# Second weighed one-hot row of every other group of eight tokens made by ScalarE, a token at a time

## The chip, the cores and the metric

The kernel runs on one core of one Trainium2 chip. The metric is the device time in microseconds of one execution, the median of the runs. Engines are called by the names of the profile: PE is TensorE (PEld its weight load), DVE is VectorE, ACT is ScalarE, POOL is GpSimd, SP is SyncE; ACTq and SPq are the queues from which ACT and SP issue transfers.

## The reference

Two blocks follow one another on 512 tokens of width 1024. What matters here is the last part of the second block, a layer of 16384 single-neuron experts, of which each token uses 128 (8 heads of 16):

```python
def peer_ffn(xn, w_q, sub_keys, u, v):
    ...
        best, pos = lax.top_k(cand, PEER_TOPK)
        expert = jnp.take_along_axis(cand_idx, pos, axis=-1)
        g = jax.nn.softmax(best, axis=-1)
        act = jax.nn.gelu(jnp.einsum('td,thkd->thk', xb, u[expert]), approximate=False)
        return jnp.einsum('thk,thkd->td', (g * act).astype(xb.dtype), v[expert])
```

An expert's number is `128 * key1 + key2`. The weight of an expert for a token is the sum of the token's `g` over its picks of that expert, and 0 where it has none.

## The kernel before

The 512 tokens stand in four tiles of 128. For one tile the experts' rows are gathered by indirect transfers. For the other three (`NDENSE`) the layer is computed densely: all 128 chunks of 128 experts, each as a projection (`u_task`, L1719 and L1722), a Gelu (L1731), a weight per expert and token (`weigh`, L1739) and a second product (`v_task`, L1766).

The weights of the dense tiles are a matrix of 16384 experts by 384 tokens, which `gate_matrix(i)` makes for tile i, four tokens at a time, and stores in the DRAM tensor `gate_d`. For a group of eight tokens, `rows` compares the picks' two keys with 0 to 127 on DVE (L1439, two instructions of 128x1024 in f16): for each pick (partition) and token a one-hot row of key 1 and one of key 2. `weighed` multiplies the rows of key 1 by the pick's weight (L1446). The weight is held as two f16 parts, `picks[i][:, 2]` and what f16 rounding left of it, `picks[i][:, 3]`, so there are two instructions, one for each part. `product` takes four tokens: for each, two matmuls of 128x128 (L1454, one for each part) add up the 128x128 matrix over key 2 and key 1 in PSUM. `store` copies the four matrices out of PSUM with two ACT instructions (L1463, called stores below) into staging tiles; after sixteen tokens two transfers bring these to `gate_d` (L1467, issued by ACT). There are 48 groups, 96 products, 192 stores and 48 transfers.

This runs in the background of the first projections: while PE does `u_task` for the first chunks, a generator is pumped. So PE's order is a projection (L1719, 16 matmuls in the trace, 8 rows in the order below), then a run of 4, 6 or 7 products, then the next projection. ACT takes the projection out of PSUM with one Gelu (L1731, `hid`). A scheduler fixes each engine's order when the program is built. In this phase projections and products take turns on the same four PSUM banks:

```python
BANKS = (dict(a=("a", 8)),
         dict(a=("a", 4), s=("s", 2), o=("o", 2), l=("o", 2), k=("o", 2)),
         dict(a=("a", 2), z=("z", 6)))
```

Roles that are not named there, `u` and `g` among them, use `a`. A projection or product that comes four places after another waits until ACT has emptied the bank. The one-hot rows use a tag of ten buffers (`sm.tile(..., tag="t", bufs=NT)`); a group holds three of them (key 2 and the two weighed parts) until PE has done its two products.

After the last store the first weights are read back (`load_gates`, L1695, issued by SP), and the dense layer goes on in other PSUM banks.

Of the kernel before, what the change touches and what calls it, by code (L numbers as in the profile page):

```python
# [7 lines left out]
F32 = mybir.dt.float32  # L8
# [4 lines left out]
AF = mybir.ActivationFunctionType  # L13
OP = mybir.AluOpType
# [155 lines left out]
def tile_kernel(ctx: ExitStack, tc: tile.TileContext, ins, out):  # L170
    nc = tc.nc
# [14 lines left out]
    def ps_tile(role="a"):  # L186
        tag, n = psum["roles"].get(role, psum["roles"]["a"])
        return psum["pool"].tile([128, 512], F32, tag=tag, bufs=n, name="ps")
# [101 lines left out]
    sm = ctx.enter_context(tc.tile_pool(name="sm", bufs=2))  # L290
# [547 lines left out]
    def second_block():  # L838
# [554 lines left out]
            def weights(i):  # L1393

                ex, best = picked.pop(i)
                ex = [ex[:, j] for j in range(2)]
                if i in idx:
                    nc.vector.scalar_tensor_tensor(out=idx[i].rearrange("p (h k) -> p h k", k=TOPK), in0=ex[0],
                                                   scalar=float(NKEY), in1=ex[1], op0=OP.mult, op1=OP.add)
                    g = gw[i].rearrange("p (h k) -> p h k", k=TOPK)  # L1400
                else:
                    g = sm.tile([128, PH, TOPK], F32, name="gwt", bufs=1)
                nc.vector.tensor_tensor(out=g, in0=best, in1=best[:, :, 0:1].to_broadcast([128, PH, TOPK]),
                                        op=OP.subtract)
                nc.scalar.activation(g, g, AF.Exp)
                sm8 = sm.tile([128, PH], F32, name="sm8", bufs=1)
                nc.vector.tensor_reduce(out=sm8, in_=g, axis=AX.X, op=OP.add)
                nc.vector.reciprocal(out=sm8, in_=sm8)
                nc.vector.tensor_tensor(out=g, in0=g, in1=sm8[:, :, None].to_broadcast([128, PH, TOPK]), op=OP.mult)
                if i in picks:  # L1410
                    p = ps_tile("g")
                    for j, x in enumerate((*ex, g)):
                        nc.tensor.transpose(p[:, j * 128:(j + 1) * 128], x.rearrange("p h k -> p (h k)"), ident)

                    x = picks[i]
                    nc.scalar.activation(x[:, :2], p[:, :256].rearrange("p (a b) -> p a b", b=128), AF.Copy)
                    nc.scalar.activation(x[:, 2], p[:, 256:384], AF.Copy, scale=WSCALE)
                    nc.vector.scalar_tensor_tensor(out=x[:, 3], in0=p[:, 256:384], scalar=WSCALE, in1=x[:, 2],
                                                   op0=OP.mult, op1=OP.subtract)
                    W.later(gate_matrix(i), name="gates")  # L1420

            def gate_matrix(i):

                k1, k2, *w = (picks[i][:, j] for j in range(4))
                full = [128, 4, 128, 2]
                keys = it16[:, None].to_broadcast(full)
                stage = []

                def wide(x, t0):
                    return x[:, t0:t0 + 8].rearrange("p (a b) -> p a b", b=2)[:, :, None, :].to_broadcast(full)  # L1430

                def row():
                    return sm.tile([128, 4, 128, 2], F16, tag="t", bufs=NT, name="oh")

                def rows(t0):

                    oh = [row() for _ in range(2)]
                    for x, k in zip(oh, (k1, k2)):
                        nc.vector.tensor_tensor(out=x, in0=keys, in1=wide(k, t0), op=OP.is_equal)  # L1439
                    return oh  # L1440

                def weighed(t0, oh):

                    parts = [row() for _ in w]
                    for x, y in zip(parts, w):
                        nc.vector.tensor_tensor(out=x, in0=oh[0], in1=wide(y, t0), op=OP.mult)  # L1446
                    return [oh[1], *parts]

                def product(t0, oh):
                    ps = ps_tile("g").rearrange("p (t n) -> p t n", n=128)  # L1450
                    for t in range(4):
                        a, b = divmod(t0 % 8 + t, 2)
                        for j in (1, 2):
                            nc.tensor.matmul(ps[:, t], oh[0][:, a, :, b], oh[j][:, a, :, b],  # L1454
                                             start=j == 1, stop=j == 2)
                    return ps

                def store(t0, ps):
                    if t0 % 16 == 0:
                        stage[:] = [W.pool.tile([128, 1024], F32, tag=tag, bufs=n, name="stage")  # L1460
                                    for tag, n in (("hi", SPLITS_AHEAD + 1), ("lo", SUBS_AHEAD + 1))]
                    for j in range(2):
                        nc.scalar.activation(  # L1463
                            stage[j].rearrange("p (n t) -> p t n", t=16)[:, t0 % 16:t0 % 16 + 4],
                            ps[:, :, j * 64:(j + 1) * 64], AF.Copy, scale=1.0 / WSCALE)
                        if t0 % 16 == 12:
                            nc.scalar.dma_start(gate_d[:, (128 * i + t0) // 16, j * 1024:(j + 1) * 1024], stage[j])  # L1467

                raw, oh, ps = {}, {}, {}
                for t0 in range(0, 128 + 12, 4):  # L1470
                    if t0 - 12 in ps:
                        store(t0 - 12, ps.pop(t0 - 12))
                    if t0 % 8 == 0 and t0 < 128:
                        raw[t0] = rows(t0)
                    if t0 - 4 in raw:
                        oh[t0 - 4] = weighed(t0 - 4, raw.pop(t0 - 4))
                    if 0 <= t0 - 8 < 128:
                        ps[t0 - 8] = product(t0 - 8, oh[(t0 - 8) // 8 * 8])
                    yield

            halves.extend([half(0), half(1)])
            n = [256]
# [70 lines left out]
            for word in PLAN.split():  # L1553
# [4 lines left out]
                else:  # L1558
                    name = word.rstrip("01234")
# [402 lines left out]
```

## Time and profile before

| | us |
|---|---|
| median of 3 runs (lowest to highest) | 3288.51 (3286.36 to 3288.88) |
| the profiled execution | 3287.23 |
| its span | 3285.5 |
| PE busy in the span | 3243.4 |
| DVE, ACT busy in the span | 2034.4, 1295.6 |

The span is the stretch from the first instruction to the last; 1.7 us of the profiled execution lie outside it. The granted clock was 0.997 of full over the span. All times of day below are microseconds from the start of the span. In a timeline a row that merges several instructions gives the first start, the time to the last end and their count, and in brackets the idle time of the engine ahead of it and what ended it.

### The profile page before, as it was taken

The numbers are of one execution on the slowest core, as the hardware profiler recorded it, in microseconds if no ns is written. First come the engines' busy times: TensorE is split into PE (matmuls) and PEld (weight loads), VectorE is DVE, ScalarE is ACT, GpSimd is POOL, SyncE is SP. The second block draws the span as 40 slices with busy tenths as digits, with TensorE's granted clock in tenths as the row PEclk, the third lists the DMA queues.
The fourth block names the chain that finished last, engine by engine and source line by source line (L and its number), as shares of the span: only waits on it lengthen the run. The fifth ranks groups of instructions, "written<-read, shape, count | busy, mean of one in ns | idle before, by whom it ended". The sixth has DMA issues, their size and how long they took to land. (4 is left out here: it accounts for less than half of the span.)

```text
span 3285.5 us, 47545 instructions
## 1 busy us (share of the span) xinstructions
PE 3243.4 (99%) x19335; PEld 2890.5 (88%) x19335; DVE 2034.4 (62%) x3979; ACT 1295.6 (39%) x2340; POOL 181.4 (6%) x132
## 2 busy tenths in 40 slices
PE   8999999999999999999999999999999999999999
PEld 7999999999888888888888988766789999999998
DVE  6545554433754555433466659988898888888443
ACT  5343332323533323232455543357433333333333
POOL 0000000000000000000000000000132222222000
PEclk9999999999999999999999999999999999999999
DMA  6222222222422222222332123356899988998442
GB/s 216 74 87 87 78 78 90 90 91 103 176 74 94 93 84 78 90 96 96 116 116 90 52 103 131 126 195 241 302 365 351 343 336 313 351 354 325 144 146 95
DMA packets 129947, 531.81 MB, mean 162 GB/s; under 512 B 9136, under 2 KB 60992, under 8 KB 73280
## 3 DMA queue, kind: packets, MB, share of 16 engines
q1 hardware_dynamic: 103520, 368.19, 31.2%
q0 software_dynamic: 18432, 134.23, 10.6%
q10 hardware_dynamic: 7776, 26.37, 2.0%
q8 instruction: 151, 2.47, 0.3%
q14 instruction: 68, 0.56, 0.1%
HBM read 501.48 MB, written 27.26 MB: 161 GB/s over the span
## 5 line engine op out<-in xcount | busy, mean ns | idle before, releaser
L143 ACT ACTIVATE hi<-raw 128x1024 fp32r<-128x1024 f32 x532 | 563.3, 1060 | 1396.5 <-PE ps L387 620.6
L151 DVE TENSOR_TENSOR lo<-raw,hi 128x1024 fp32r<-128x1024 f32 x532 | 650.8, 1224 | 744.8 <-ACT hi L143 741.2
L387 PE MATMUL ps<-xnh,hi 128*128 128x256 f32 (+2 forms) x2080 | 511.4, 305 | 0.0
L387 PE MATMUL ps<-xnl,hi 128*128 128x256 f32 (+2 forms) x2080 | 510.3, 305 | 0.0
L387 PE MATMUL ps<-xnh,lo 128*128 128x256 f32 (+2 forms) x2080 | 508.9, 304 | 0.0
L1766 PE MATMUL ps<-hi,hw 128*128 128x512 f32 x1536 | 428.4, 394 | 3.5 <-ACT hid L1731 2.8
L1722 PE MATMUL ps<-hn,hi 128*128 128x384 f32 x1600 | 409.5, 337 | 0.0
L387 PEld LDWEIGHTS ps<-xnh,hi 128*128 128x128 f32 x2080 | 338.9, 188 | 18.0
L387 PEld LDWEIGHTS ps<-xnh,lo 128*128 128x128 f32 x2080 | 339.4, 189 | 17.1
L387 PEld LDWEIGHTS ps<-xnl,hi 128*128 128x128 f32 x2080 | 338.5, 188 | 15.9
L1766 PEld LDWEIGHTS ps<-hi,hw 128*128 128x128 f32 x1536 | 288.5, 189 | 64.2 <-ACT hid L1731 3.4
L1636 POOL DMA_INDIRECT uv<-uv,idx x128 | 181.1, 1415 | 2842.6 <-DVE hn L1596 2328.6
L1722 PEld LDWEIGHTS ps<-hn,hi 128*128 128x128 f32 x1600 | 290.8, 188 | 4.3
L1722 PE MATMUL ps<-hn,lo 128*128 128x384 f32 x800 | 269.2, 337 | 0.0
L1766 PE MATMUL ps<-lo,hw 128*128 128x512 f32 x768 | 240.2, 393 | 0.0
L1766 PEld LDWEIGHTS ps<-lo,hw 128*128 128x128 f32 x768 | 145.0, 189 | 32.4
L1664 DVE SCALAR_TENSOR_TENSOR acc<-uv,dots,acc 128x1024 f32<-128x1024 f32 x127 | 163.0, 1284 | 3.2
L1672 DVE SCALAR_TENSOR_TENSOR uv<-uv,hnT 128x1024 f32<-128x1024 f32 x128 | 155.9, 1219 | 11.7 <-DMA uv<-uv,idx 11.7
L1719 PE MATMUL ps<-hn,raw 128*128 128x384 f32 x448 | 149.6, 490 | 5.5 <-ACT stage L1463 4.9
L1722 PEld LDWEIGHTS ps<-hn,lo 128*128 128x128 f32 x800 | 150.0, 188 | 0.1
L888 PE MATMUL ps<-x,hi 128*128 128x256 f32 x768 | 140.9, 287 | 4.0 <-ACT x L274 3.4
L1719 PEld LDWEIGHTS ps<-hn,raw 128*128 128x128 f32 x448 | 83.4, 190 | 63.3 <-ACT stage L1463 8.2
(353 smaller groups left out, 5036.8 us busy)
## 6 DMA issues: line engine op xcount, KB each, us to landing
raw<-ws SPq DMA_DIRECT2D x313, 1024.0 KB, 4.8
gate_d<-stage ACTq DMA_DIRECT2D x48, 512.0 KB, 3.5
gates<-gate_d SPq DMA_DIRECT2D x16, 1536.0 KB, 13.1
dm<-decay_m SPq DMA_DIRECT2D x8, 264.0 KB, 5.3
vb<-vbias SPq DMA_DIRECT2D x8, 256.0 KB, 5.6
dc<-decay SPq DMA_DIRECT2D x8, 256.0 KB, 5.4
uv<-uv,idx POOLq DMA_INDIRECT x128, 8.3
h<-ht SPq DMA_DIRECT2D x2, 544.0 KB, 5.0
```

The lines of the kernel that those rows point to most:

```text
L143: nc.scalar.activation(hi, raw[i], AF.Copy)
L151: nc.vector.tensor_tensor(out=lo, in0=r, in1=parts[i][0].bitcast(F32), op=OP.subtract)
L387: nc.tensor.matmul(t[:, :b - a], w[wi][:, off + k, :], x[k].t[xi][:, a:b], start=(k == 0 and n == 0), stop=(k == K - 1 and n == 2))
L888: nc.tensor.matmul(p, parts[wi][:, k, :], x[k][:, xi], start=(k == 0 and n == 0), stop=(k == K - 1 and n == 2))
L1636: nc.gpsimd.indirect_dma_start(out=t, out_offset=None, in_=ins["uv"], in_offset=bass.IndirectOffsetOnAxis(ap=idx[i][:, j:j + 1], axis=0))
L1664: nc.vector.scalar_tensor_tensor(out=acc, in0=v, scalar=dots[:, j:j + 1], in1=acc, op0=OP.mult, op1=OP.add)
L1672: nc.vector.scalar_tensor_tensor(out=u, in0=u, scalar=1.0, in1=hnT, op0=OP.mult, op1=OP.mult, accum_out=dots[:, j:j + 1])
L1719: nc.tensor.matmul(ps, w[0][:, k, :], tl["hn32"][k][:, :ND], start=k == 0, stop=k == KD - 1)
L1722: nc.tensor.matmul(ps, w[wi][:, k, :], tl["hn"][k][:, xi], start=(k == 0 and n == 0), stop=(k == KD - 1 and n == 2))
L1766: mm = nc.tensor.matmul(tl["acc"][t][b], h[:, hi, t * 128:(t + 1) * 128], w[vi][:, b * 512:(b + 1) * 512], start=(e == 0 and n == 0), stop ...
```

## The change

For every second group of eight tokens (`t0 % 16` is 8 when `weighed` is called with the group's first token) the second of the two multiplications leaves DVE. In its place ACT runs eight instructions, one for each token, on 128x128 elements that lie two apart, each a copy scaled by that token's column of weights: a scale that differs from partition to partition. The scale is read from `rest`, an f32 copy of the second weight part, which ACT makes once for each token tile. So 24 DVE instructions go and 192 + 3 ACT instructions come.

```diff
@@ -1422,6 +1422,8 @@
                 k1, k2, *w = (picks[i][:, j] for j in range(4))
+                rest = sm.tile([128, 128], F32, name="rest")
+                nc.scalar.activation(rest, w[1], AF.Copy)
                 full = [128, 4, 128, 2]
@@ -1442,8 +1444,13 @@
                 def weighed(t0, oh):
 
                     parts = [row() for _ in w]
-                    for x, y in zip(parts, w):
-                        nc.vector.tensor_tensor(out=x, in0=oh[0], in1=wide(y, t0), op=OP.mult)
+                    for n, (x, y) in enumerate(zip(parts, w)):
+                        if n and t0 % 16:
+                            for t in range(8):
+                                nc.scalar.activation(x[:, t // 2, :, t % 2], oh[0][:, t // 2, :, t % 2], AF.Copy,
+                                                     scale=rest[:, t0 + t:t0 + t + 1])
+                        else:
+                            nc.vector.tensor_tensor(out=x, in0=oh[0], in1=wide(y, t0), op=OP.mult)
                     return [oh[1], *parts]
```

The scheduler places the new instructions. Lines shift by seven: the stores are L1470 after the change, `hid` is L1738, the transfers are L1474, the new instructions L1450. Two places on ACT and one on DVE are shown.

The first is ACT's order in the third token tile, from the projection ahead of products 76 to 82 (counted from 0 over the three tiles) to the next one. Before, it read:

```order
L1731 ACTIVATE hid<-ps 128x384
L1463 ACTIVATE stage<-ps 128x4x64 x10
L1467 DMA gate_d<-stage 128x1024 x2
L1463 ACTIVATE stage<-ps 128x4x64 x2
L1731 ACTIVATE hid<-ps 128x384
```

With the change the same piece reads:

```order
L1738 ACTIVATE hid<-ps 128x384
L1470 ACTIVATE stage<-ps 128x4x64 x4
L1450 ACTIVATE oh<-oh,rest 128x128 x6
L1470 ACTIVATE stage<-ps 128x4x64 x2
L1450 ACTIVATE oh<-oh,rest 128x128 x2
L1470 ACTIVATE stage<-ps 128x4x64 x8
L1474 DMA gate_d<-stage 128x1024 x2
L1450 ACTIVATE oh<-oh,rest 128x128 x8
L1738 ACTIVATE hid<-ps 128x384
```

Eight of the new instructions stand between the first four stores and the last eight, and eight more behind these. Twelve stores became fourteen because PE now has all of the seventh product ahead of the next projection, where it had one of its eight matmuls.

The second is ACT's order in the first token tile, between the projections ahead of and behind products 15 to 21, with the change. Sixteen of the new instructions stand here, all behind the tenth store:

```order
L1738 ACTIVATE hid<-ps 128x384
L1470 ACTIVATE stage<-ps 128x4x64 x2
L1474 DMA gate_d<-stage 128x1024 x2
L1470 ACTIVATE stage<-ps 128x4x64 x8
L1450 ACTIVATE oh<-oh,rest 128x128 x4
L1470 ACTIVATE stage<-ps 128x4x64 x2
L1450 ACTIVATE oh<-oh,rest 128x128 x4
L1470 ACTIVATE stage<-ps 128x4x64 x2
L1474 DMA gate_d<-stage 128x1024 x2
L1450 ACTIVATE oh<-oh,rest 128x128 x8
L1738 ACTIVATE hid<-ps 128x384
```

Before, that stretch held sixteen stores and two pairs of transfers between its two `hid` rows, with nothing else between them.

The third is DVE's order near the end of the third token tile, with the change. Two comparisons and then two multiplications used to repeat for every group:

```order
L1441 TENSOR_TENSOR oh<-it_100,picks_104 128x1024 x2
L1453 TENSOR_TENSOR oh<-oh,picks_104 128x1024 x2
L1441 TENSOR_TENSOR oh<-it_100,picks_104 128x1024 x2
L1453 TENSOR_TENSOR oh<-oh,picks_104 128x1024
```

Every second pair of multiplications is now a single one, and nothing else moved.

## Rows read from the trace of the kernel before

**Rows 1.** The page's first part: busy time, share, instructions of PE.
```profile
PE 3243.4 (99%) x19335; PEld 2890.5 (88%) x19335; DVE 2034.4 (62%) x3979; ACT 1295.6 (39%) x2340; POOL 181.4 (6%) x132
```

**Rows 2.** Windows: the last two token tiles' products, and what follows to the dense layer.
```profile
2206.71:2294.31 87.60, 79.94 (x641) 56.64 (x640) 70.29 (x120) 60.05 (x130) 0.00 (x0) 1.00 0.61 231
2294.31:2318.04 23.73, 20.91 (x64) 12.08 (x64) 20.23 (x61) 15.40 (x28) 0.00 (x0) 0.98 0.83 285
```

**Rows 3.** Waits from 2140 to 2296: us in total, times, longest.
```profile
ACT hid L1731 <- PE ps L1719: 40.6, 15, 3.7
DVE oh L1439 <- PE ps L1454: 21.9, 13, 2.2
PE ps L1454 <- ACT stage L1463: 5.5, 17, 1.2
PE ps L1719 <- ACT stage L1463: 4.9, 12, 0.7
PE ps L1454 <- DVE oh L1439: 1.5, 6, 0.3
```

**Rows 4.** Timeline of PE, a run of six products and one of seven.
```profile
2206.71 2.46 PE L1454 MATMUL ps<-oh 128*128 128x128 f16 x40
...
2210.31 5.43 PE L1719 MATMUL ps<-hn,raw 128*128 128x384 f32 x16 [0.28 <-ACT stage L1463]
2215.57 2.49 PE L1454 MATMUL ps<-oh 128*128 128x128 f16 x40
...
2220.03 5.43 PE L1719 MATMUL ps<-hn,raw 128*128 128x384 f32 x16 [0.66 <-ACT stage L1463]
2225.30 2.42 PE L1454 MATMUL ps<-oh 128*128 128x128 f16 x39
```

**Rows 5.** Timeline of ACT beside the first of these runs.
```profile
2206.91 0.49 ACT L1731 ACTIVATE hid<-ps 128x384 f32<-128x384 f32 x1 [0.68 <-PE ps L1719]
2207.38 1.98 ACT L1463 ACTIVATE stage<-ps 128x256 f32<-128x256 f32 x4
...
2209.57 3.34 ACT L1463 ACTIVATE stage<-ps 128x256 f32<-128x256 f32 x7
...
2215.77 0.49 ACT L1731 ACTIVATE hid<-ps 128x384 f32<-128x384 f32 x1 [2.86 <-PE ps L1719]
```

**Rows 6.** Groups by line on ACT from 1600 to 2320: busy us, mean ns.
```profile
L143 ACT ACTIVATE hi<-raw 128x1024 fp32r<-128x1024 f32 x53 | 55.8, 1057 | 103.4 <-PE ps L888 60.3 <-PE ps L1276 23.7 <-DMA raw<-ws 9.5
...
L216 ACT ACTIVATE r<-ms,eps 128x8 f32<-128x8 f32 x4 | 1.2, 301 | 0.0
...
L1405 ACT ACTIVATE gwt<-gwt 128x128 f32<-128x128 f32 x3 | 0.9, 304 | 0.0
L1135 ACT ACTIVATE r<-r 128x8 f32<-128x8 f32 x4 | 0.8, 208 | 0.1
```

**Rows 7.** Timeline of ACT, three short instructions that follow one another.
```profile
2106.56 0.27 ACT L1417 ACTIVATE picks<-ps 128x128 f16<-128x128 f32 x1
2106.72 0.31 ACT L1405 ACTIVATE gwt<-gwt 128x128 f32<-128x128 f32 x1
2106.93 0.37 ACT L1176 ACTIVATE early<-ps 128x256 f32<-128x256 f32 x1
```

**Rows 8.** Groups by line on DVE from 1600 to 2400: the multiplications.
```profile
L1446 DVE TENSOR_TENSOR oh<-oh,picks 128x1024 f16<-128x1024 f16 x96 | 62.0, 686 | 0.0
```

**Rows 9.** Chain that ended last, in order of time, from the last stores on.
```profile
2296.53 2.64 DMA gate_d<-stage
...
2299.24 9.07 DMA gates<-gate_d
...
2308.34 2.55 DVE hid L1739 x6
...
2317.61 0.39 ACT hid L1731
...
2318.04 11.31 PE ps L1766 x36
```

## The prediction

> **What bounds the kernel now.** I began with the page's busy times: PE works 3243.4 of 3285.5 us [rows 1], so whatever makes PE wait longer goes straight to the end, and a change off PE can win back at most the 42 us in which it is idle. The change touches the phase in which the weights are made, so I asked for the windows of that phase. From 2206.71 to 2294.31, the last two token tiles, PE is busy 79.94 of 87.60 us, DVE 70.29, ACT 60.05 [rows 2]. DVE looks like the busier helper. The waits say otherwise: from 2140 to 2296 PE waits 5.5 + 4.9 = 10.4 us for ACT's stores, and 1.5 us for DVE's rows; DVE waits 21.9 us for PE to free its buffers, and ACT 40.6 us for projections to end [rows 3]. So DVE has room, and ACT delays PE although it is idle a third of the time. The timelines show why. ACT's stores come in a row behind each `hid`, one every 0.445 us ((3.34 - 0.67) / 6 with about 0.67 for the last), while PE fills four tokens' bank in 0.5 us (2.49 / 5). PE takes the banks in turn. With six products between projections, the next projection needs the bank of the third, which the sixth store empties; with seven, that of the fourth, and the eighth store. By the rows: `hid` at 2206.91, first store 0.47 later, sixth store five steps of 0.44 after that, 0.66 to end it, and the projection starts at 2210.31: 0.2 + 0.47 + 2.2 + 0.66 + 0.07 = 3.60 us after the run began, as seen. For seven products 0.2 + 0.47 + 3.08 + 0.73 = 4.48, seen 4.46 (2215.57 to 2220.03) [rows 4, 5]. Only the stores up to that one, which I call the deciding store, are on the path. The later ones run beside the projection (about 5.26 us from its start to the next run's, 2210.31 to 2215.57), and behind them ACT is idle for 2.86 us, which is the room that new work on ACT can have for nothing [rows 5].
>
> **What the change costs, part by part.** It takes 24 of the 96 multiplications from DVE, 24 x 62.0 / 96 = 15.5 us [rows 8]. PE hardly waits for DVE, so this is worth nothing, bounded by the 1.5 us.
>
> It gives ACT 192 scaled copies of 128x128. None is in the trace. The nearest row by shape and place is the Exp from SBUF to SBUF of 128x128, 304 ns [rows 6], after which the next instruction starts 0.21 us later (2106.72 to 2106.93) [rows 7]. That has no operand that differs by partition. What such an operand costs is seen on 128x8: 301 ns with one (L216, its bias), 208 without (L1135) [rows 6], 93 ns. So one lasts about 397 ns, and in a row of eight, of which each starts about 0.1 us ahead of the other's end, one comes every 0.30 us. The bounds: 0.16 us, the shortest step between rows of this size (L1417 to L1405, 2106.56 to 2106.72) [rows 7], and 0.40 us if nothing overlaps. I take 0.30, since the row nearest in kind carries that operand. [...]
>
> Now what of it lies on the path. In the order, I count the new instructions that stand ahead of the deciding store of each of the seventeen runs of products: none in eleven of them; 8 for products 9 to 14, 8 for 40 to 46, 8 for 53 to 59, 6 for 64 to 69, 8 for 76 to 82 (the first place shown), and 8 for 89 to 95. That is 46, and each holds up the stores behind it on ACT, and these the next projection: 46 x 0.30 = 13.8 us. In the other runs the new instructions stand behind the deciding store. There they cost nothing where they fit into the idle 2.86 us: eight take 2.4 us. At the second place shown sixteen stand there. Fourteen stores end 0.2 + 0.47 + 14 x 0.44 = 6.83 us after the run began, sixteen copies bring that to 11.63, while the projection ends at 4.48 + 5.26 = 9.74 and its `hid` could start at 9.94. So `hid` and the stores behind it are 1.7 us late, and the next run, of six, waits that long at its deciding store. With the delayed runs the projection starts later too, so that their eight behind (0.2 + 0.47 + 14 x 0.44 + 16 x 0.30 = 11.63 against 4.48 + 2.4 + 5.26 + 0.2 = 12.34) still fit. One spill therefore, 1.7 us.
>
> The rows that the copies read are DVE's, three groups ahead by the ten buffers, and DVE is lighter; I take no wait for them. The three copies into `rest` wait on ACT for DVE's second weight part. For the first two, `hid` waits behind them, and the cover is the run of projections ahead of the first products: with four banks PE notices nothing. Without that cover they would cost 2 to 4 us once. The first eight scaled copies have the same cover.
>
> Last, the end of the phase. PE waits for `hid` at 2318.04, and the chain leads back over the reading of the weights (9.07 us), the last transfer of stores at 2296.53, and ACT [rows 9]. From PE's last products on, that chain is 23.73 us long with PE busy 20.91 [rows 2], so nothing covers a delay. With the change the split of a weight piece (L143, `hi`) stands ahead of the store that this transfer waits for; before, it stood behind it. That is 1.06 us by its row [rows 6] if nothing else waits for it; I take 1.0, between 0 and 1.9 (the split and two stores more).
>
> The sum is 13.8 + 1.7 + 1.0 = 16.5 us, on the profiled execution's 3287.23: 3303.7. The median of the runs is 1.3 us above that execution; I round to 3304 us, 0.5% slower.
>
> **Rivals.** (a) *The copies fall into ACT's idle time or are short.* For it: 40.6 us of idle time on ACT [rows 3] against 192 x 0.16 = 31 us at the lower bound. Then 46 x 0.16 = 7.4 and no spill: 3295; with less on the path than I counted, 3290 to 3294. Against it: the operand's 93 ns, and the place of the 46.
> (b) *ACT becomes the bound throughout.* At 0.40 us a copy, 46 cost 18.4; the spill of sixteen grows to 3.3, and the runs for which eight just fitted spill by 0.1 to 1.1 each, about 2.2 together; with 1.9 at the end that is 25.8: 3313. For it: no row shows that copies with such an operand overlap, and elements two apart may cost more. In the stretch of 87.60 us [rows 2] ACT would have 60.05 us of old work and 112 of the copies, 45 us, 105 in all, in a stretch that (with 38 of the 46) the deciding stores alone would make 87.6 + 15.2 = 103 long; at 0.30 it is 94 of 99.
> (c) *Faster, because DVE sets the pace.* DVE is the busier of the two in rows 2, and its 21.9 us of waiting may be the loop of buffers between it and PE and no slack. Freed of 15.5 us it would run ahead, PE would find every run's rows and banks ready, and all of PE's waits in the phase would go, 5.5 + 4.9 + 1.5 = 11.9 us: 3275. It decides if the stores are late because products are, that is if ACT's `hid` has nothing queued behind it when PE waits. Against it: the 0.445 us step of the stores accounts for both runs to within 0.02 us.
>
> **How the numbers follow.** Chances: the forecast, steps of 0.25 to 0.35 us with the 46 on the path, 0.50; (b) 0.22; (a) 0.24; (c) 0.04. The forecast's own range is 3300 to 3307 (46 x 0.25 + 1 to 46 x 0.35 + 2.5 + 1). The range for 8 in 10 reaches from 3295, (a)'s lower bound, to 3313, (b)'s. About what a measurement of this kernel tells from no change is 0.2%, 6.6 us: 3282 to 3295. Half of (a), 0.12, lies within it; (c) alone lies below, 0.04; the rest, 0.84, is slower.
>
> **What would show it.** Right: the new rows (L1450) at 0.39 to 0.41 us each, some 0.30 apart; PE's waits for stores (10.4 us before) at about 25; runs of seven products such as 76 to 82 at 12 us in place of 9.7; those of six with the copies behind, 8.9 as before; DVE's waits for PE longer. Wrong: L1450 rows starting under 0.2 us apart; PE waiting for DVE's rows or for L1450 itself, which would mean that a product waits for its second part; `hid` late in nearly every run, which is (b); or a phase as long as before, which is (a).

## The result and the profile after

The changed kernel takes 3310.75 us (median; 3306.4 to 3311.46) against 3288.24 (3286.36 to 3288.88) for the kernel before beside it: ratio 1.0072, 95% interval 1.0059 to 1.0085. The forecast was 3304 with a range of its own, 3300 to 3307, and one for 8 in 10, 3295 to 3313; the median lies within the second and above the first. The profiled execution of the changed kernel took 3306.40 us with a span of 3304.6 and a granted clock of 0.996; the other runs have 0.993 to 0.994 and are 4 to 5 us longer.

First the page's busy times of the changed kernel, to be held against [rows 1]:

```profile
PE 3246.6 (98%) x19335; PEld 2892.9 (88%) x19335; DVE 2020.4 (61%) x3955; ACT 1348.3 (41%) x2535; POOL 187.4 (6%) x132
```

DVE lost 14.0 us, ACT gained 52.7, PE's busy time rose by 3.2 with the same matmuls. The last of these is the first sign of something that the forecast did not have.

The phase, as a window from the first product to the start of the last projections (1044 matmuls in both). Columns: stretch, its length, busy time of PE, of weight loads, DVE, ACT, POOL (instructions), granted clock, DMA share, GB/s. Before:

```profile
2140.78:2294.31 153.53, 140.63 (x1044) 97.45 (x1043) 128.82 (x310) 99.03 (x223) 0.00 (x0) 1.00 0.57 214
```

After:

```profile
2140.41:2313.51 173.10, 145.12 (x1044) 100.35 (x1042) 115.95 (x288) 149.50 (x408) 0.00 (x0) 0.97 0.50 190
```

This phase holds the loss: it is 19.57 us longer, where the two profiled executions as wholes differ by 19.17 (the end of the phase adds 0.8, and the stretches ahead of the phase and behind its end are 1.3 us shorter). PE's idle time went from 12.90 to 27.98 us, +15.1; its busy time rose by 4.5 at a clock of 0.97. The waits of the changed kernel from 2140 to 2316 (us in total, times, longest) say where the 15.1 come from:

```profile
DVE oh L1441 <- ACT oh L1450: 26.4, 7, 4.9
...
DVE oh L1453 <- ACT oh L1450: 19.7, 8, 3.2
PE ps L1461 <- ACT stage L1470: 16.5, 19, 1.9
ACT hid L1738 <- PE ps L1726: 10.7, 12, 2.2
...
DVE oh L1441 <- PE ps L1461: 6.7, 6, 1.9
PE ps L1726 <- ACT stage L1470: 6.6, 13, 1.9
...
PE ps L1461 <- ACT hid L1738: 2.7, 3, 2.0
...
PE ps L1726 <- ACT hid L1738: 1.8, 1, 1.8
...
PE ps L1461 <- DVE oh L1441: 0.3, 1, 0.3
```

PE waits for stores 16.5 + 6.6 = 23.1 us (10.4 in [rows 3]), for `hid` 4.5 (0.7 before), for DVE's rows 0.3 (1.8): 12.7 + 3.8 - 1.5 = 15.0. It never waits for a copy. DVE now waits 26.4 + 19.7 = 46.1 us for ACT to read its rows, and 6.7 in place of 21.9 for PE; almost none of it reaches the products.

One place, PE's timeline for products 40 to 46 (the run at 2215.57 of [rows 4]):

```profile
2221.69 2.50 PE L1461 MATMUL ps<-oh 128*128 128x128 f16 x40
2224.37 0.63 PE L1461 MATMUL ps<-oh 128*128 128x128 f16 x8 [0.18 <-ACT stage L1470]
2226.92 0.63 PE L1461 MATMUL ps<-oh 128*128 128x128 f16 x8 [1.92 <-ACT stage L1470]
2228.31 6.93 PE L1726 MATMUL ps<-hn,raw 128*128 128x384 f32 x16 [0.76 <-ACT stage L1470]
2235.07 1.10 PE L1461 MATMUL ps<-oh 128*128 128x128 f16 x16
```

And ACT's beside it:

```profile
2221.89 0.49 ACT L1738 ACTIVATE hid<-ps 128x384 f32<-128x384 f32 x1 [0.65 <-PE ps L1726]
2222.36 1.97 ACT L1470 ACTIVATE stage<-ps 128x256 f32<-128x256 f32 x4
2224.11 1.87 ACT L1450 ACTIVATE oh<-oh,rest 128x128 f16<-128x128 f16 x6
2225.84 1.03 ACT L1470 ACTIVATE stage<-ps 128x256 f32<-128x256 f32 x2
2226.66 0.70 ACT L1450 ACTIVATE oh<-oh,rest 128x128 f16<-128x128 f16 x2
2227.22 1.03 ACT L1470 ACTIVATE stage<-ps 128x256 f32<-128x256 f32 x2
```

The fifth and seventh store stand behind six and two copies; PE waits 1.92 us for the sixth store and 0.76 for the eighth. The run lasts 6.62 us in place of 4.46. Then the projection, with nothing to wait for, takes 6.93 us instead of 5.43. The window of that projection shows why: a granted clock of 0.77, where the phase before had 1.00.

```profile
2228.31:2235.07 6.76, 6.76 (x16) 3.85 (x17) 0.69 (x1) 4.76 (x14) 0.00 (x0) 0.77 0.40 158
```

The copies themselves, by their line (minimum, median and maximum in ns):

```profile
L1450 ACT ACTIVATE oh<-oh,rest x192: 397/427/466, 2111.2 to 2310.3; 128x128 f16<-128x128 f16 x192
```

A row of eight lasts 2.44 us, so one comes every (2.44 - 0.40) / 7 = 0.29 us.

### The profile page after: what moved, and what is told of

The parts are those of the page before. It is cut to its first block, busy times and chain, and to the rows that moved or that the text cites. A ratio compares the mean times of both kernels' runs of the same rounds, so it can differ in the third digit from the quotient of the medians.

```text
span 3304.6 us, 47730 instructions
## 1 busy us (share of the span) xinstructions
PE 3246.6 (98%) x19335; PEld 2892.9 (88%) x19335; DVE 2020.4 (61%) x3955; ACT 1348.3 (41%) x2535; POOL 187.4 (6%) x132
## 5 line engine op out<-in xcount | busy, mean ns | idle before, releaser
L143 ACT ACTIVATE hi<-raw 128x1024 fp32r<-128x1024 f32 x532 | 563.3, 1060 | 1405.3 <-PE ps L387 620.6
```

The costliest lines, as they stand in the source:

```text
L143: nc.scalar.activation(hi, raw[i], AF.Copy)
```

## The experiments

In this section each run's ratio is taken to the kernel before as it ran beside it. Theory 1 is the forecast's mechanism: a copy costs what it takes where it stands ahead of a deciding store (or of a `hid`) in ACT's order, and nothing elsewhere; the falls of the clock behind PE's longer waits were added to it from the trace after. Rival 1: ACT's occupancy costs, wherever the copies stand. Rival 2: products wait for second parts that come late. Rival 3: DVE sets the pace, so that its relief is worth something.

**Only the copies ahead.** (8 i + t0 // 16 numbers the 24 changed groups.)

```
-  if n and t0 % 16:
+  if n and t0 % 16 and 8 * i + t0 // 16 in (3, 11, 14, 17, 20, 23):
```

> Only six of the 24 multiplications go to ACT, those whose copies stand ahead of the deciding stores (46 of their 48 copies do, counted in the order); the other eighteen stay on DVE. Theory 1 (what stands ahead of a deciding store in ACT's row is paid in full, the rest is not): nearly the whole loss of the change, 46 x 0.29 = 13.3 us, about 3 us of falls of TensorE's clock behind the longer waits and 0.9 at the end: ratio 1.0052, about 3305 us (3301 to 3309). Rival 1 (ACT's occupancy costs, wherever the copies stand): a quarter of the measured 22.5 us, 3294 us, ratio 1.0017. Rival 2 (the products wait for second parts that come late): a quarter too, 3294 us, and waits of PE for the copies' rows.

Measured: 3304.55 us, ratio 1.0053 (1.0038 to 1.0067): a quarter of the copies makes three quarters of the loss. Rivals 1 and 2 fall by their number. The phase's window:

```profile
2140.89:2314.75 173.86, 150.54 (x1044) 102.61 (x1043) 125.38 (x302) 112.65 (x272) 0.00 (x0) 0.93 0.50 189
```

PE's idle time is 23.3 us, 10.4 more than before; its busy time is 9.9 more. So the clock took as much as the waits in this execution. The timeline of PE at products 40 to 46:

```profile
2221.96 0.63 PE L1461 MATMUL ps<-oh 128*128 128x128 f16 x8 [0.21 <-ACT stage L1470]
2224.50 0.62 PE L1461 MATMUL ps<-oh 128*128 128x128 f16 x8 [1.92 <-ACT stage L1470]
2225.89 8.49 PE L1726 MATMUL ps<-hn,raw 128*128 128x384 f32 x16 [0.77 <-ACT stage L1470]
```

The same waits as in the changed kernel, and behind them a projection of 8.49 us (clock 0.63 from 2225.89 to 2234.20), where the changed kernel had 6.93 at the same place. How deep the clock falls behind such waits differs from place to place and from run to run, while the waits repeat to 0.02 us. One line of this run's waits speaks for another cause:

```profile
PE ps L1461 <- DVE oh L1453: 4.0, 3, 1.9
```

Two of these three are 1.88 and 1.87 us long and stand at the places (2163.52 and 2248.03) where the changed kernel waits 1.87 and 1.86 for a store. ACT's store and DVE's row end there within 0.1 us of one another, so at these two places a store that comes earlier would have gained next to nothing without an earlier row.

**Only copies behind.**

```
-  if n and t0 % 16:
+  if n and t0 % 16 and 8 * i + t0 // 16 not in (0, 1, 3, 11, 14, 17, 20, 23):
```

> The counterpart: sixteen of the 24 multiplications go to ACT, those whose copies stand behind the deciding store of their run; the six ahead of it, and the first two of the first tile (whose copies stand ahead of the hid of a projection), stay on DVE. 128 copies, two thirds of ACT's new work. Theory 1: about the time of the kernel before, 3288 us (3285 to 3292), ratio 1.000 (to 1.001 for a spill behind sixteen copies). Rival 1 (occupancy): two thirds of 22.5 us, 3303 us, ratio 1.0046. Rival 3 (a lighter DVE is worth something): 16 x 0.65 = 10.3 us less on DVE, up to 3 us faster, 3285 us or less.

Measured: 3288.52 us, ratio 1.0008 (0.9999 to 1.0018). Two thirds of the new work on ACT cost nothing that can be measured. The phase's window:

```profile
2142.24:2296.84 154.60, 141.10 (x1044) 97.69 (x1042) 119.73 (x292) 134.66 (x352) 0.00 (x0) 1.00 0.56 213
```

ACT is busy 35.6 us longer than before, PE idle 0.6 longer, and the clock stays at 1.00. Rival 1 is refuted for this amount of work.

**DVE's relief alone.** This is an edit of the kernel before. In the odd groups the second part is left out, and PE uses the first one twice. Such a group holds two of the ten buffers in place of three, so DVE is relieved a little more than by the change.

```
-  parts = [row() for _ in w]
-  for x, y in zip(parts, w):
-      nc.vector.tensor_tensor(out=x, in0=oh[0], in1=wide(y, t0), op=OP.mult)
+  parts = [row() for _ in w[:1 if t0 % 16 else 2]] * (2 if t0 % 16 else 1)
+  for n, (x, y) in enumerate(zip(parts, w)):
+      if n and t0 % 16:
+          parts[1] = parts[0]
+      else:
+          nc.vector.tensor_tensor(out=x, in0=oh[0], in1=wide(y, t0), op=OP.mult)
```

> DVE's relief alone: in every other eight tokens the second part of the weight is left out (the first part's rows are multiplied twice, so PE has as many matmuls as before), DVE makes 24 multiplications fewer, and ACT gets nothing new. Theory 1: PE hardly waits for DVE, so about the time before, 3288 us (3286 to 3290), at best the 1.8 us that PE waited for DVE's rows. Rival 3 (DVE sets the pace of this phase): 24 x 0.65 us less, up to 3275 us, ratio 0.996. If the former holds, the change had nothing to win even with copies that cost nothing.

Measured: 3287.2 us, ratio 1.0007 (0.9998 to 1.0016). The change had nothing to win that can be measured, whatever its copies cost. DVE, 14 us lighter in the phase, waits longer for its buffers (21.9 us in [rows 3]; window 2140 to 2298):

```profile
DVE oh L1449 <- PE ps L1457: 35.4, 14, 3.7
...
PE ps L1457 <- ACT stage L1466: 7.4, 19, 1.1
```

PE waits 0.6 us for DVE's rows here (1.8 before) and 11.0 for stores (10.4 before).

**A shorter copy in the same place.** The second parts lose their weight (all are 0 or 1).

```
-  scale=rest[:, t0 + t:t0 + t + 1])
+  scale=1.0)
```

> The changed kernel with a constant 1.0 in place of the scale that differs by partition (the weight is left out of those second parts); all copies stay where they are. Theory 1: a copy lasts about 0.30 us and comes every 0.20 instead of 0.294 us, so 46 x 0.09 = 4.2 us less on the path, 0.7 less at the two hid, and shorter single waits (8 x 0.2 = 1.6 instead of 2.4 us), behind which the clock falls less often: 3302 us (3298 to 3307), ratio about 1.0045. If the copies cost by their place and not by their length, or wait on memory: as the changed kernel, 3310 us, ratio 1.007.

Measured: 3301.39 us, ratio 1.0043 (1.0029 to 1.0057). ACT's timeline for products 40 to 46 again:

```profile
2223.01 1.99 ACT L1470 ACTIVATE stage<-ps 128x256 f32<-128x256 f32 x4
2224.78 1.33 ACT L1450 ACTIVATE oh<-oh 128x128 f16<-128x128 f16 x6
2225.97 1.03 ACT L1470 ACTIVATE stage<-ps 128x256 f32<-128x256 f32 x2
2226.80 0.54 ACT L1450 ACTIVATE oh<-oh 128x128 f16<-128x128 f16 x2
```

The order is the same, a copy comes every (1.33 - 0.34) / 5 = 0.20 us, and the operand that differs by partition is the other 0.09 of 0.29, near the 93 ns between L216 and L1135 in [rows 6]. PE's wait in this run is 1.39 us in place of 1.92, and the projection behind it takes 5.43 us: no fall here. The execution has one fall, behind products 2 to 8 (a projection of 7.49 us).

**The copies beside the multiplications.** This too is an edit of the kernel before. DVE makes all multiplications, and ACT copies into a tile that nobody reads.

```
+  rest = sm.tile([128, 128], F32, name="rest", bufs=1)
+  nc.scalar.activation(rest, w[1], AF.Copy)
...
   nc.vector.tensor_tensor(out=x, in0=oh[0], in1=wide(y, t0), op=OP.mult)
+  if n and t0 % 16:
+      spare = sm.tile([128, 128, 2], F16, name="spare", bufs=1)
+      for t in range(8):
+          nc.scalar.activation(spare[:, :, t % 2], oh[0][:, t // 2, :, t % 2], AF.Copy,
+                               scale=rest[:, t0 + t:t0 + t + 1])
```

> DVE makes all 96 multiplications again, as before the change, and ACT makes the 192 scaled copies beside them, into a spare tile that nobody reads. The same new work on ACT, but no product waits for it. Since nothing hangs on the copies, they stand elsewhere in ACT's order: 26 of them ahead of deciding stores (3, 3, 4, 4, 4, 4, 4 in seven runs), where the change had 46, and never more than four in one run. Theory 1: 26 x 0.29 = 7.5 us and about 0.9 at the end, single waits of about 1 us longer, too short for falls of the clock: 3296 us (3293 to 3299), ratio 1.0025. Rival 1 (occupancy of ACT, wherever it stands): as the changed kernel, 3310, ratio 1.007. Rival 2 (products that wait for late second parts): 3288, ratio 1.000.

Measured: 3302.03 us, ratio 1.0049 (1.0035 to 1.0063), 17 us where theory 1 said 8 and the others 0 or 22. Rival 2 falls: no product reads these copies, PE waits for DVE's rows as long as before (1.7 us), and the copies cost 17. But my count for theory 1 was too low. The profiled execution is the shortest (3299.10 us), and its phase is 12.0 us longer than before; three of the other four have a granted clock of 0.995 against 0.997 and take 3302 to 3304 us. ACT's timeline shows what the count lacked:

```profile
2167.38 3.25 ACT L1452 ACTIVATE spare<-oh,rest 128x128 f16<-128x128 f16 x10
2170.50 0.46 ACT L1738 ACTIVATE hid<-ps 128x384 f32<-128x384 f32 x1
2170.87 1.05 ACT L1470 ACTIVATE stage<-ps 128x256 f32<-128x256 f32 x2
```

Ten copies stand behind the stores here, on top of single ones among them, and `hid` comes without a pause, 0.4 us later than its projection would have let it (PE's next run began at 2169.86, and a `hid` can follow 0.2 us after: 2206.71 and 2206.91 in [rows 4, 5]). ACT waits for projections 4.2 us in this phase (six times) where it waited 40.6 before [rows 3]. So the room behind the stores was used up in most runs, and late `hid` are a part of the loss; how much each part took I did not separate. Here occupancy does count, past the room that each run leaves; that a copy behind then costs as much as one ahead was not measured. (PE's longest wait for a store is 1.41 us, and the phase's clock is 1.00 in this execution. That waits of this length are too short for falls was an estimate; with the whole change on the quick stores, below, projections of 7.12 us stand behind waits of 1.18 and 1.24 us.)

**Fewer, faster or moved stores.** If stores decide, a kernel with quicker ones should beat both. The first try merges a product's two stores:

```
-  for j in range(2):
-      nc.scalar.activation(stage[j].rearrange("p (n t) -> p t n", t=16)[:, t0 % 16:t0 % 16 + 4],
-                           ps[:, :, j * 64:(j + 1) * 64], AF.Copy, scale=1.0 / WSCALE)
+  nc.scalar.activation(stage[0].rearrange("p (n t) -> p t n", t=8)[:, t0 % 8:t0 % 8 + 4],
+                       ps, AF.Copy, scale=1.0 / WSCALE)
...
-  nc.sync.dma_start(t, gate_d[:, :, g * 128:(g + 1) * 128])
+  nc.sync.dma_start(t, gate_d[:, :, g * 64:(g + 1) * 64])
```

> The kernel before with one store for each product in place of two (both halves of the experts at once, 128x512, into a stage of eight tokens; gates are kept by eights of tokens in DRAM, so that a load of them has pieces of 256 B in place of 512 B). The deciding store is then the third or fourth one, about 0.65 us each (between 0.49 us for a hid of 128x384 and 1.06 for a split of 128x1024): 0.2 + 0.47 + 2 x 0.62 + 0.7 = 2.6 us after the run began, when PE needs 3.0 for its six products. Theory 1: most of the 10.4 us that PE waits for stores goes: 3279 us (3277 to 3283), ratio 0.9972. If the load of the gates, which stands in the chain that ends this phase, takes longer by its smaller pieces (9.07 us before), up to 8 us of that are given back: 3287. Rival 3 (DVE sets the pace): 70.3 us of DVE's work against 87.6 - 8 leave room, but if it binds, PE waits for DVE's rows instead and the gain is 3 us or less.

Measured: 3300.74 us, ratio 1.0044 (1.003 to 1.0057), slower. ACT's groups by line show the store that I had at 0.7 us:

```profile
L1462 ACT ACTIVATE stage<-ps 128x512 f32<-128x512 f32 x96 | 94.0, 1161 | 0.1
```

Twice the elements take twice as long (a step of (3.05 - 1.16) / 2 = 0.94 us in the timeline, against 0.44), so a store pays by the element, 1.7 to 1.8 ns each, where a `hid` of 384 takes 490 ns in all. The deciding store comes no earlier: a run of six waits 3.76 us for its projection (2207.99 to 2211.75) in place of 3.60, and PE's waits for stores add up to 16.7 us (10.4 before).

These waits are the smaller part of the loss. The windows of the phase, and of the stretch from the first of the second products (`v_task`) to the last instruction, which was 967.46 us long before:

```profile
2140.25:2299.29 159.04, 141.26 (x1044) 97.52 (x1042) 128.17 (x306) 103.73 (x130) 0.00 (x0) 1.00 0.55 210
2321.43:3299.00 977.57, 957.24 (x4770) 857.81 (x4768) 728.06 (x1033) 359.85 (x612) 174.74 (x128) 1.00 0.82 284
```

The phase is 5.5 us longer and the last projections between the two 1.6 shorter, but the dense layer behind them is 10.1 longer. There PE waits 13.5 us for ACT's splits of the weights (L143), where it did not wait for them before:

```profile
PE ps L1764 <- ACT hi L143: 13.5, 9, 1.6
```

That layer reads the gates in pieces of 256 B here; whether this delays the splits was not tested. So the run shows that one store for two does not shorten the waits; the 15.7 us by which it is slower than the kernel before beside it (3285.0) are not the price of the store alone.

The same on top of the change:

> The changed kernel with that same single store. Some 46 copies still stand ahead of deciding stores (7 or 8 in each of six runs). A run of six then has its deciding store done 0.2 + 0.47 + 1.24 + 0.7 + 8 x 0.294 = 5.0 us after it began in place of 3.0 that PE needs, 2.0 us late in each of six runs: theory 1 says 12 us slower than the single store alone, and 1 to 6 us more by falls of the clock: about 3293 us (3289 to 3299). If occupancy mattered, the freed 26 us of ACT's stores would pay for half of the copies' 56 us, and it would come near the single store alone plus 11 us at no fixed place. If DVE binds with the single store, the relief shows here, and it comes out within 3 us of the single store alone.

Measured: 3329.34 us, ratio 1.0132 (1.0117 to 1.0148), 28.6 us above the single store alone, more than the 13 to 18 expected. The waits are near the expected size (2.23 to 2.26 us in six runs, expected 2.0), but the granted clock of these runs is 0.991 to 0.992, with six projections of 6.0 to 8.1 us in the profiled execution. In this execution 24.0 of the 28.6 us lie in the phase.

The second stores of every other product on DVE:

```
+  if j and t0 % 8 == 0:
+      nc.vector.tensor_scalar(out=x, in0=y, scalar1=1.0 / WSCALE, scalar2=None, op0=OP.mult)
+  else:
       nc.scalar.activation(x, y, AF.Copy, scale=1.0 / WSCALE)
```

> The kernel before with the second store of every other product made by DVE (a multiplication by the constant from PSUM), the contrary direction to the change: ACT is relieved by 48 stores, DVE has 48 instructions of 128x256 more. Theory 1: one or two fewer stores of 0.44 us stand ahead of the deciding one in each run, so PE waits 0.4 to 0.9 us less where it waits now: 3282 us (3279 to 3286), ratio 0.9982. Against it: DVE takes its instructions in order too, so a store that waits for its product holds up the next rows; where DVE is not far enough ahead, PE waits for rows instead: 3288 to 3296.

Measured: 3294.36 us, ratio 1.0029 (1.002 to 1.0039). The profiled execution took 3302.23 us, 8 above the median, and 7.0 us of its loss lie in the phase. PE waits longer for ACT's stores there (9.1 + 7.1 us), although there are fewer. ACT itself now stands waiting for DVE ahead of `hid` (4.0 + 3.2 us) and for products (7.0 us); I did not take this further.

**The loops of a store swapped.** Each expert's four tokens are written side by side.

```
-  stage[j].rearrange("p (n t) -> p t n", t=16)[:, t0 % 16:t0 % 16 + 4],
-  ps[:, :, j * 64:(j + 1) * 64], AF.Copy, scale=1.0 / WSCALE)
+  stage[j].rearrange("p (n t) -> p n t", t=16)[:, :, t0 % 16:t0 % 16 + 4],
+  ps.rearrange("p t n -> p n t")[:, j * 64:(j + 1) * 64], AF.Copy, scale=1.0 / WSCALE)
```

> The kernel before, with the two loops of a store (tokens and experts) in the other order: the four tokens of an expert are written side by side (16 B at a time) and read 512 B apart, where before each element was written 64 B from the last. Same elements, same places, same numbers of instructions. A store of 256 with the old order comes every 0.44 us, a contiguous row of 256 (L1416) every 0.26 us; the single store of 512 came every 0.94, so the cost is by the element and not by the instruction. If it is the distance of the writes that costs: about 0.28 us, the deciding store done 0.2 + 0.47 + 5 x 0.28 + 0.45 = 2.5 us after the run began, when PE needs 3.0; the 10.4 us of waits go: 3279 us (3277 to 3283), ratio 0.9972. If the distance of the reads costs as much: 3288 us, ratio 1.000, or slower.

Measured: 3271.77 us, ratio 0.996 (0.9947 to 0.9974): faster than both kernels. ACT's timeline:

```profile
2218.36 0.49 ACT L1731 ACTIVATE hid<-ps 128x384 f32<-128x384 f32 x1 [4.25 <-PE ps L1719]
2218.77 1.21 ACT L1463 ACTIVATE stage<-ps 128x256 f32<-128x256 f32 x4
```

A store comes every (1.21 - 0.41) / 3 = 0.27 us. The phase's window:

```profile
2140.56:2279.28 138.72, 136.15 (x1044) 96.61 (x1043) 128.11 (x305) 67.66 (x223) 0.00 (x0) 1.00 0.61 235
```

It is 14.8 us shorter; PE is idle for 2.6 us of it. Its busy time fell too, by 4.5, since eight matmuls that start anew after a pause show 0.62 us, and eight of a row that goes through 0.49 (48 in 2.96). In these runs elements written 64 and 32 B apart cost 1.7 and 1.8 ns each (0.44 us / 256, 0.94 / 512), elements written four side by side about 1.05 (0.27 us / 256).

The same arrangement made by PE, which writes tokens side by side into the bank:

```
-  ps = ps_tile("g").rearrange("p (t n) -> p t n", n=128)
+  ps = ps_tile("g").rearrange("p (n t) -> p n t", t=4)
...
-  nc.tensor.matmul(ps[:, t], oh[0][:, a, :, b], oh[j][:, a, :, b],
+  nc.tensor.matmul(ps[:, :, t], oh[0][:, a, :, b], oh[j][:, a, :, b],
...
-  stage[j].rearrange("p (n t) -> p t n", t=16)[:, t0 % 16:t0 % 16 + 4],
-  ps[:, :, j * 64:(j + 1) * 64], AF.Copy, scale=1.0 / WSCALE)
+  stage[j].rearrange("p (n t) -> p n t", t=16)[:, :, t0 % 16:t0 % 16 + 4],
+  ps[:, j * 64:(j + 1) * 64], AF.Copy, scale=1.0 / WSCALE)
```

> As that, but with PE writing each token's 128 experts 16 B apart into the bank, so that a store reads it contiguously and writes 16 B at a time. If only the distances on ACT's side cost: at least as good as the swapped loops, 3279 us (3277 to 3283), and better than they if reads 512 B apart cost. If PE is slowed by writing apart (128 columns in 62 ns before: eight matmuls each 0.5 us), 96 products of 0.5 us may take up to twice as long, 3288 + 48 - 10 = 3326.

Measured: 3300.99 us, ratio 1.0052 (1.0039 to 1.0066). PE's timeline of a run of six products:

```profile
2211.49 5.40 PE L1454 MATMUL ps<-oh 128*128 128x128 f16 x48
```

That is 112 ns a matmul, where 40 took 2.49 us (62 ns) in [rows 4]. PE never waits for a store there, and pays for it with every product. ACT's reads of PSUM 512 B apart, in the swapped loops, show no such loss: a store comes every 0.27 us there, and every 0.27 us (0.66 for two, 0.39 for one) here, where it reads side by side and writes the same way.

**The change on top of the quick stores**, whole and with the copies behind only:

> The changed kernel with the swapped store loops (0.28 us a store). ACT's order is the same as in the changed kernel: 46 copies ahead of deciding stores, eight ahead of each of two hid. ACT now has some 30 us more room than in the kernel before. Theory 1: the room does not help, since what counts is the place. In six runs the deciding store is 2.35 us later (1.76 in one) against the 0.43 us by which it came ahead of PE's need: 5 x 1.92 + 1.33 = 10.9 us; 3 us for the two hid, 0.9 at the end, 3 to 6 by falls of the clock behind waits of 1.9 us: 3271.8 + 20 = 3291 us (3286 to 3297), ratio 1.002. Rival 1 (occupancy): the copies' 56 us are half paid for, 3271.8 + 10 = 3282 us or less. If ACT was late only because its stores were slow: 3272 to 3276.

> The swapped store loops with those sixteen multiplications on ACT whose copies stand behind the deciding stores. Theory 1: as the swapped loops alone, 3271.8 us (3269 to 3275), ratio 0.996; the 10.3 us less on DVE is worth at most the 1.1 us that PE still waits for its rows. Rival 3 (with the stores out of the way DVE sets the pace): 3268 us or less. Rival 1 (occupancy): some 10 us more than the swapped loops alone, 3282.

Measured: with the whole change 3292.62 us, ratio 1.0017 (1.0008 to 1.0025); with the copies behind 3271.94, ratio 0.9966 (0.9953 to 0.9978), the same as the swapped loops alone. The price of the whole change is 20.9 us here and 22.5 there, although ACT was given 31 us of room in the phase. Two windows, whole:

```profile
2140.07:2299.22 159.15, 143.14 (x1044) 100.17 (x1042) 115.48 (x283) 120.64 (x408) 0.00 (x0) 0.97 0.54 206
```

and the copies behind:

```profile
2140.16:2279.19 139.03, 136.37 (x1044) 96.71 (x1043) 119.28 (x289) 105.13 (x352) 0.00 (x0) 1.00 0.61 234
```

ACT is busy 105 of 139 us in the second, and PE idle 2.7. In the first the falls of the clock are back: PE works 7.0 us longer than with the swapped loops alone, in part by rows that start anew, in part by two projections of 7.12 us in place of 5.43 and 32 matmuls of 3.57 us in place of 2.02. Two of its waits, 1.24 us each, end with a row of DVE that lands within 0.1 us of the store, so with quick stores DVE's rows are close behind. (This profiled execution, 3298.52 us, is 5.9 above its median.)

## Why the prediction was right, and where its terms were off

The mechanism held in the runs that test its steps one by one: DVE's relief is worth nothing; a copy costs where it stands ahead of a deciding store; copies behind cost nothing while they fit. As a count of microseconds it did worse where the order or the stores changed too: the unread copies, the single store, that store with the change, the stores on DVE and the transposed products came out slower than theory 1 said, and the swapped loops faster. The terms of the sum, in the profiled execution:

- **46 copies ahead, 13.8 us.** Measured 12.7 as PE's added wait for stores, with half of the spill in it (the other half is a wait of 0.57 us for `hid`). Runs with eight copies ahead grew by 2.15 us (4.46 to 6.62, 6.61 and 6.63), the one with six by 1.64 (3.60 to 5.24): 0.27 us a copy. The copy's length, 0.397 by the sum, was 0.397 at the least and 0.427 at the median; the step, 0.30, was 0.29.
- **One spill, 1.7 us.** It is there: the `hid` behind the sixteen copies started at 2185.28, 1.4 us later than its projection would have let it, and the run of six behind it took 4.86 us in place of 3.67, 1.2 more.
- **End of the phase, 1.0 us.** The split (L143) does stand ahead of the last stores in the chain, and from PE's last products on the chain is 24.53 us long (23.73 before): 0.8.
- **The first copies, nothing.** This step was wrong. I had them covered by the projections ahead of the first products. Two `hid` came late in the first tile, and PE waited 3.8 us more for `hid`, 0.6 of them by the spill:

```profile
2142.69 0.23 ACT L1359 ACTIVATE mf<-m 128x32 f32<-128x32 uint32 x1 [0.77 <-DVE m L1357]
2142.83 0.47 ACT L1738 ACTIVATE hid<-ps 128x384 f32<-128x384 f32 x1
...
2150.52 2.44 ACT L1450 ACTIVATE oh<-oh,rest 128x128 f16<-128x128 f16 x8
2152.84 0.47 ACT L1738 ACTIVATE hid<-ps 128x384 f32<-128x384 f32 x1
```

The second of them stands directly behind eight copies; PE waited 1.95 us for it. The first stands behind no copy: the new order put an instruction that waits for DVE (L1359) ahead of it, where `hid` came first before, and PE waited 1.84 us in place of 0.51. That a changed order can move old instructions too had no term. Without those copies (the run with copies behind only) PE waits 1.1 us for `hid` in all.
- **No term for the clock.** Missing altogether. PE's added busy time in the phase is 4.5 us here, 9.9 in the run with the copies ahead only; of the 4.5, three stretches carry 4.6 (the projections at 2228.31 and 2268.75, 1.5 and 1.7 longer, and 32 matmuls at 2153.36, 3.43 us in place of 2.02). The other three executions of the changed kernel have a lower granted clock (0.993 to 0.994) and are 4 to 5 us longer still. That more falls make up this difference fits their clock, but is not shown: only one execution has a trace.

So the forecast of 3304 was near the profiled 3306.4 in part by luck, because errors offset each other: 3.8 and 4.5 us were missing, while the copies with their spill were put 2.8 too high, PE's wait for DVE's rows, put at no change, fell by 1.5, and the rest of the span came out 1.3 shorter. The median, 3310.75, lies above the forecast's own range (3300 to 3307); it is covered only by the room up to 3313 that was left for rival (b), which is not what happened. Of the rivals, (a) is out by the run with the copies ahead only: they are not in ACT's idle time. (b), ACT as the bound throughout, is out since two thirds of the copies cost nothing; the run with unread copies shows that it begins soon past that. (c) is refuted by the relief alone. Of the right signs, the rows' length and step, PE's waits for stores (23.1 us for 25) and the runs (76 to 82 with the projection behind it 11.90 us, those of six 8.9) came near; DVE's waits for PE, which should have been longer, fell from 21.9 to 6.7, since DVE waits for ACT to read its rows instead. The wrong signs did not show, except `hid` late for PE at three places.

What remains open: what decides how far the clock falls behind a wait. In these traces the falls stand behind waits of 1.2 to 2.3 us, most with a second wait close by, and not behind every such wait: in the changed kernel the projection behind waits of 1.92 and 0.76 us took 6.93 us (2228.31), and the one behind 1.92 and 0.77 took 5.43 (2291.19). In the kernel before the phase's clock is 1.00.

## What to carry to other kernels

An engine that is idle a third of the time can still be the wrong place for new work: count, in its order, what will stand ahead of the instruction for which the bounding engine waits, and charge that in full; charge nothing for what stands behind and fits into the pause there. Look then at how that instruction spends its time. Here the stores paid for the distance of their writes in SBUF (0.44 us each at 64 B, 0.27 with four elements side by side), and swapping two loops was worth more (13 us) than any division of the work that was tried. Look, too, at which old instructions a new order moves. And where PE's waits grow, add a term for its clock, as uncertain as the waits are certain (here 4.5 us of added busy time with the change, 9.9 with the copies ahead only, at clocks of 0.97 and 0.93).

## What the hardware showed unexpectedly

- ACT's store of 256 elements takes 0.44 us a step when each 4-byte element is written 64 B from the last, 0.27 when four are side by side and the reads are 512 B apart in PSUM; 512 elements written 32 B apart take 0.94. The copies, 2-byte elements 4 B apart, show none of it (0.20 us for 128 with a constant scale; an Exp of 128 side by side has 0.21 in [rows 7]).
- PE's matmul of 128 columns takes 112 ns when it writes its columns 16 B apart into PSUM, 62 ns when side by side.
- Behind waits of 1.2 to 2.3 us within a busy phase some projections took 6.0 to 8.5 us in place of 5.43; the granted clock was 0.62 to 0.77 in the five whose window was read.
